# A hybrid layer in one kernel: the pass boundary rewritten (held mLSTM outputs, kept tiles chosen by chain state, output weights through the weight ring, attention banks dealt anew)

## The chip, the cores and the metric

The kernel runs on 1 core of a Trainium2 chip. The metric is the device time of one execution in microseconds. A profiled execution also leaves a trace of the five engines: TensorE (PE, with its weight loads shown as PEld), VectorE (DVE), ScalarE (ACT), GpSimd (POOL), and SyncE (SP), which here only issues DMA transfers. L243 means line 243 of the kernel's file.

## The reference

One layer over 2,048 positions of width 1,024, all in float32. The input is normalised, and one projection gives the columns of three head groups. Each group's output is gated; the three are joined, projected back, added to the input, and normalised.

```
hn = rmsnorm(x, norm_g)
z  = einsum('bsd,de->bse', hn, w_in)            # split among three groups
att   = band_chunk_attention(aq, ak, av, rel_bias)   # 6 heads, own 64-chunk and 8 before it
y_a   = att * silu(ag)
h_ml  = mlstm_chunkwise(silu(conv(mq)), silu(conv(mk)), mv, mi, mf)   # 6 heads, matrix memory
y_b   = sigmoid(mo) * head_rmsnorm(h_ml) * silu(mg)
h_gla = gla_chunkwise(gq, gk, gv, log_alpha)         # 4 heads, gated linear attention
y_c   = head_rmsnorm(h_gla) * silu(gg)
x     = x + einsum('bse,ed->bsd', concat(y_a, y_b, y_c), w_out)
return rmsnorm(x, final_g)
```

The mLSTM group carries a matrix state from chunk to chunk. Its output is divided by a normaliser, normalised per head, and multiplied by the gate `gm` (sigmoid(mo) * silu(mg)).

## The kernel before, in words

**Arithmetic.** Large products use split operands: each float32 operand is held as a high part (a rounded `fp32r` copy, made by ACT) and a low part (the difference, made by DVE or POOL), and three matmuls stand for one: high x high, high x low, low x high. So a projection tile (`proj_g`, L239) is 8 x 3 = 24 matmuls of 128x128 against 512 columns, L243 to L245. `load_w` (L229) brings one tile's weights through the raw ring `wraws` (2 buffers of 512 KB) into the split ring `wring` (5 buffers).

**Pass A** (L757 to L788) walks over four blocks of 512 positions. Each block projects in a fixed order: `gq`, `gk`, two groups of four `proj_t` tiles with `gg` between, six tiles for the mLSTM's q and k (`proj_m`), six for its gates (`proj_gm`), and nine for attention (`proj_a`: q, k and gate, three each). Attention's q, k, v and gate go to DRAM (`q_d`, `k_d`, `v_d`, `ga_d`), and so do the outputs of mLSTM and GLA (`y_d`, row tiles 3 to 7).

TensorE's order is written out by the program. Between the projection's matmuls it calls `flow.piece(12 * 0.227)`, and the planner `Flow` (L33) then steps the chains that are due: generators that issue some TensorE work and yield its cost and the gap after which the next step is due. `flow.need(name)` steps chains with no projection between, until the named one has ended. The other engines' order is chosen by the compiler's scheduler, across the whole program.

The chain `mlstm` (L521) handles four chunks of 128 positions per block. Per chunk: decay matmuls (L532, cost 0.7, gap 4.5), scores and key transposes (L542, L546; 1.0, gap 4.5), then output and state update (L560, L565, L577), the normalisation on DVE and POOL (L589 to L602; 1.7, gap 9), and last the output's transposes (L611) and the product with `gm` (L613), then the store L614 (0.35, gap 1). The next chunk begins only after that. In the last block, attention tiles 5 to 8 are not projected but kept (L507); then `need("gla")` and `need("mlstm")` (L787) finish the chains.

**Pass B** (from L791). `attention(q)` yields steps of `scores` (L844: per row tile up to two segments, L868, then the masked sum and row minimum on DVE, L882, the exponential on ACT, L885, the scaling on POOL, L887) and of `mix` (L901: transposes L932 into bank `tp`, the high and low copies `ph` L937 and `pl` L938, and the products with v, L946 and L949, in bank `w`, evacuated by L953 and L954). `merge` interleaves two generators in a given ratio. The mix of a head lags its scores by two heads in block 0 and by one later.

`proj_kept` (L512) projects the four kept tiles between the first 32 steps of block 0's attention. Then `load_wo` (L812) closes the projection's pools, opens the pool `late` on the same memory, and loads the output weights in 16 halves with four raw buffers, together with block 0's row tiles 3 to 7 of y; each is split by L839 (ACT) and L840 (DVE or POOL). Its 21 steps alternate with the 28 that remain of block 0's attention.

After that, for blocks 1 to 3, `spread` mixes the attention of block q with `out_mm(q - 1)` (L978): 64 pieces of three matmuls (L990 to L992), then residual and final norm. Block 1's attention takes its first eight steps alone. At the end of a block `load_y` (L1010, L1012) loads the next five row tiles through the four raw buffers and splits them (L897, L898). `out_mm(3)` runs alone at the end.

PSUM has eight banks: in pass B two each for `s`, `tp`, `w` and `ip`.

Of the kernel before, what the change touches and what calls it, by code (L numbers as in the profile page):

```python
# [104 lines left out]
def trunk_kernel(ctx: ExitStack, tc: tile.TileContext, xT, x, w_f, w_t, w_o, w_gates, norm_g, conv_w,  # L105
# [36 lines left out]
    with ExitStack() as pa_:  # L142
# [378 lines left out]
        def mlstm(q, qk, vs, R):  # L521
            rt, iwl = R["rt"], R["iwl"]
            for c in range(NC):
# [77 lines left out]
                hb = m_tile([P, 3, 2, 64])  # L601
                nc.vector.tensor_tensor(hb.rearrange("p a b d -> p b a d"), ov[:, :, :, 0:64],  # L602
                                        sm[:, 3].unsqueeze(3).broadcast_to([P, 2, 3, 64]), op=ALU.mult)
                hf = hb.rearrange("p a b d -> p (a b d)")
                yield 1.7, 9.0 if c < NC - 1 or q == NQ - 1 else 17.0
                while "gm" not in R:
                    yield 0.0, 1.0
                gm = R["gm"]
                ht_ps = bank("mt")
                for p in range(3):  # L610
                    nc.tensor.transpose(out=ht_ps[:, p * P:(p + 1) * P], in_=hf[:, p * P:(p + 1) * P], identity=ident)  # L611
                hbt = m_tile([P, 3, P])
                nc.vector.tensor_tensor(hbt, ht_ps[:, 0:384].rearrange("p (a t) -> p a t", a=3), gm[:, :, cs], op=ALU.mult)  # L613
                nc.sync.dma_start(y_d[q, :, 3:6, cs], hbt)  # L614
                yield 0.35, 1.0
# [141 lines left out]
        for q in range(NQ):  # L757
# [19 lines left out]
            flow.start("mlstm", mlstm(q, qk, vs, M))  # L777
# [9 lines left out]
        flow.need("gla")  # L787
        flow.need("mlstm")  # L788


    with ExitStack() as pb_:  # L791
# [4 lines left out]

        def pbank(tag):
            return (psum_i if tag == "ip" else psum).tile([P, 512], FP32, name=tag)
# [11 lines left out]
        late = {}  # L810

        def load_wo(Y):  # L812
            lag = []
            pg_.close()
            late["p"] = ctx.enter_context(tc.tile_pool(name="late", bufs=2, reuse_waits="tile"))
            late["fg"] = fg = late["p"].tile([P, D], FP32, name="fg", bufs=1)
            wo = late["wo"] = {}
            for j in range(2):
                for k in (3, 4, 5, 6, 7, 0, 1, 2):
                    raw = late["p"].tile([P, 512], FP32, name="wraw", bufs=4)  # L820
                    nc.sync.dma_start(raw, w_o[k][:, 512 * j:512 * j + 512])
                    w = wo[k, j] = late["p"].tile([P, 2, 512], FR, name="wo", bufs=2 * KT)
                    lag.append((w, raw, other()))
                    if len(lag) > 2:
                        split_late(*lag.pop(0))
                    yield
                    if j == 0 and k >= 3:
                        raw = late["p"].tile([P, QT], FP32, name="wraw", bufs=4)
                        nc.sync.dma_start(raw, y_d[0, :, k, :])
                        Y[k] = y_tile(k)  # L830
                        lag.append((Y[k], raw, nc.gpsimd))
                        split_late(*lag.pop(0))
                        yield
            for e in lag:
                split_late(*e)
            nc.sync.dma_start(fg, final_g.partition_broadcast(P))
# [7 lines left out]
        def scores(q, h, out_):  # L844
# [13 lines left out]
            for tt in range(NC):  # L858
# [7 lines left out]
                for l in range(2):  # L866
                    for sp, (c0, cn) in zip(sps, segs):
                        nc.tensor.matmul(sp[:, :cn], qq[:, l, tt * P:(tt + 1) * P], kk[:, ko + c0:ko + c0 + cn],  # L868
                                         start=(l == 0), stop=(l == 1))
                if q == 0:  # L870
# [21 lines left out]
        def y_tile(k):  # L892
            return (big if k < 3 else late["p"]).tile([P, 2, QT], FR, name="y", bufs=6 if k < 3 else 5)

        def split_y(src, k):
            yk = y_tile(k)
# [4 lines left out]
        def mix(q, h, Y, vv, pts, nkb):  # L901
# [39 lines left out]
            def pv(pr, pp, g, pk, last, ph, pl):  # L941
                if g == 0:
                    ops[pr] = pbank("w")
                op = ops[pr]
                for e, (b, use, w) in enumerate(pk):
                    nc.tensor.matmul(op[:, use[0] * P:use[0] * P + P * len(use)], vv[:, b, :], ph[:, w:w + P * len(use)],  # L946
                                     start=(g == 0 and e == 0), stop=False, skip_group_check=True)
# [3 lines left out]
                if last:  # L951
                    ps_ = slice(pr * ST, (pr + 1) * ST)
                    nc.scalar.copy(cc[mr, ps_], op[cr, :ST])  # L953
                    nc.vector.tensor_tensor(cc[mr, ps_], op[mr, :ST], cc[mr, ps_], op=ALU.add)  # L954

            held = []
            for it in todo:
                ph, pl = turn_(*it)
                yield
                if held:  # L960
                    pv(*held.pop())
                    yield
                held.append(it + (ph, pl))
            pv(*held.pop())
            if h % 2 == 1:
                nc.gpsimd.tensor_tensor(cc, cc, gt, op=ALU.mult)
                Y[h // 2] = split_y(cc, h // 2)
            yield

        def attention(q, Y):  # L970
            lag, nb = (2, 6) if q == 0 else (1, 14)
            done = []
            for h in range(AH + lag):
                a = scores(q, h, done) if h < AH else None
                b = mix(q, h - lag, Y, *done[h - lag]) if h >= lag else None
                yield from merge(a, b, NC, nb)

        def out_mm(q, Y):  # L978
            wo, fg = late["wo"], late["fg"]
            for tt in range(NC):  # L980
                t = slice(tt * P, (tt + 1) * P)
                ts_ = slice(q * QT + tt * P, q * QT + (tt + 1) * P)
                xr = late["p"].tile([P, D], FP32, name="xr", bufs=2)
                nc.sync.dma_start(xr, x[ts_, :])
                sm = big.tile([P, 4], FP32, name="sm4")
                for j in range(2):
# [9 lines left out]
                    jk = late["p"].tile([P, 512], FP32, name="jk", bufs=1)  # L996
# [122 lines left out]
```

## Time and profile before

| what | us |
|---|---|
| median of 3 runs | 1363.43 (1361.69 to 1365.0) |
| profiled execution | 1360.25 |
| its span on the core | 1358.5 |
| DVE busy in the span | 815.6 |
| ACT busy in the span | 600.7 |
| POOL busy in the span | 628.4 |
| start of the output product of block 0 | 1017.94 |

The span is the time between the first and last instruction that the trace shows; the execution's own time lies 1.75 us above it. The page cuts the span into 40 slices of 34 us and gives each engine's busy share in tenths, and the TensorE clock that was granted:

```profile
PE   4999999999999999999999999996979999999997
PEclk7999999999999999999999999997959999989999
```

Slices are counted from 0. Slices 27 to 29 (918 to 1020 us) are the boundary between the passes; the first and the last slice are the start and the end of the kernel.

### The profile page before, as it was taken

To read this page: it belongs to the slowest core of one execution; us is meant where nothing else is said; L and a number is where in the kernel's file an instruction comes from. 1 tells how busy PE (TensorE), PEld (TensorE's weight loads), DVE (VectorE), ACT (ScalarE), POOL (GpSimd) and SP (SyncE) were. 2 spreads that over 40 slices of the span, in tenths; PEclk is the share of its full clock that TensorE was granted. 3 is DMA by queue.
4 is the path that set the end of the run, shared out by engine and by line. 5 is a ranking of instruction groups with operands and counts; after the bars stand their busy time and mean duration, and the time that the engine had idled before them with its cause. 6 is when DMAs were issued, how large, how long until landed. Compare 5 with 4: busy or idle time off the path is not lost.

```text
span 1358.5 us, 19994 instructions
## 1 busy us (share of the span) xinstructions
PE 1289.8 (95%) x7044; PEld 1045.6 (77%) x7044; DVE 815.6 (60%) x1886; ACT 600.7 (44%) x1149; POOL 628.4 (46%) x847
## 2 busy tenths in 40 slices
PE   4999999999999999999999999996979999999997
PEld 2787878877777888778787877885758877877886
DVE  6626656573866575475768356555657756656631
ACT  5624332563523274342336344222566645645531
POOL 5236751333964244468333476522364353454442
PEclk7999999999999999999999999997959999989999
DMA  7444224624323563422352642332695554464222
GB/s 244 151 125 138 83 88 134 230 74 139 109 77 109 138 215 113 133 76 82 125 137 68 189 135 70 99 104 80 173 285 176 173 174 150 142 192 132 78 86 77
DMA packets 107204, 180.09 MB, mean 133 GB/s; under 512 B 9824, under 2 KB 54752, under 8 KB 107104
## 3 DMA queue, kind: packets, MB, share of 16 engines
q1 hardware_dynamic: 102496, 170.43, 41.6%
q10 hardware_dynamic: 4608, 8.39, 1.7%
q8 instruction: 55, 0.90, 0.3%
q14 instruction: 45, 0.37, 0.1%
HBM read 143.14 MB, written 35.65 MB: 132 GB/s over the span
## 4 chain that ended last, share of the span: by engine, by line
PE 76%; DVE 10%; DMA 5%; ACT 4%; issue 3%; POOL 2%; SPq 0%; POOLq 0%; DVEq 0%; ACTq 0%
PE ip L243 13%; PE ip L245 12%; PE ip L244 12%; PE ip L263 3%; PE ip L265 3%; PE ip L264 3%; PE ip L992 3%; PE ip L990 3%; PE ip L991 3%; PE s L868 3%; PE tp L932 2%; DVE pt L882 2%; PE ga L696 2%; PE w L949 2%; PE s L565 1%
## 5 line engine op out<-in xcount | busy, mean ns | idle before, releaser
L243 PE MATMUL ip<-x,w 128*128 128x512 f32 x800 | 328.0, 410 | 0.0
L245 PE MATMUL ip<-x,w 128*128 128x512 f32 x800 | 313.5, 392 | 0.0
L244 PE MATMUL ip<-x,w 128*128 128x512 f32 x800 | 312.7, 391 | 0.0
L243 PEld LDWEIGHTS ip<-x,w 128*128 128x128 f32 x800 | 150.7, 188 | 43.2 <-issue 13.9
L245 PEld LDWEIGHTS ip<-x,w 128*128 128x128 f32 x800 | 150.4, 188 | 33.2
L244 PEld LDWEIGHTS ip<-x,w 128*128 128x128 f32 x800 | 150.9, 189 | 29.6 <-issue 2.2
L236 DVE TENSOR_TENSOR w<-wraw,w 128x1024 fp32r<-128x1024 f32 x88 | 123.2, 1400 | 81.3 <-ACT w L235 80.8
L235 ACT CAST w<-wraw 128x1024 fp32r<-128x1024 f32 x132 | 138.0, 1046 | 67.1 <-DMA wraw<-in_w_t 30.7
L236 POOL TENSOR_TENSOR w<-wraw,w 128x1024 fp32r<-128x1024 f32 x44 | 106.8, 2428 | 80.5 <-ACT w L235 80.5
L887 POOL TENSOR_SCALAR pt<-pt,sm 128x640 f32<-128x640 f32 (+2 forms) x96 | 70.4, 735 | 146.4 <-DVE sm L886 115.3
L990 PE MATMUL ip<-wo,y 128*128 128x512 f32 x256 | 106.6, 416 | 0.0
L263 PE MATMUL ip<-w,x 128*128 128x512 f32 x256 | 101.3, 396 | 4.2 <-ACT vg L427 4.2
L885 ACT ACTIVATE pt<-pt,sm 128x640 f32<-128x640 f32 (+2 forms) x96 | 73.3, 763 | 69.6 <-DVE sm L882 67.1
L656 POOL TENSOR_TENSOR prd<-gk,zg 128x16 f32<-128x16 f32 (+15 forms) x128 | 73.8, 576 | 64.0 <-PE pw L662 57.8
L992 PE MATMUL ip<-wo,y 128*128 128x512 f32 x256 | 101.1, 395 | 0.3 <-POOL y L898 0.3
L991 PE MATMUL ip<-wo,y 128*128 128x512 f32 x256 | 101.1, 395 | 0.0
L265 PE MATMUL ip<-w,x 128*128 128x512 f32 x256 | 99.8, 390 | 0.0
L264 PE MATMUL ip<-w,x 128*128 128x512 f32 x256 | 99.7, 390 | 0.0
L938 DVE TENSOR_TENSOR pl<-tp,ph 128x512 fp32r<-128x512 f32 (+2 forms) x126 | 74.6, 598 | 31.3 <-ACT ph L937 29.9
L868 PE MATMUL s<-kk,qq 128*128 128x384 f32 (+1 forms) x360 | 81.5, 335 | 10.0 <-DVE sm L882 7.9
L868 PEld LDWEIGHTS s<-kk,qq 128*128 128x128 f32 x360 | 60.8, 202 | 29.2 <-DVE sm L882 23.2
L398 ACT ACTIVATE e<-ip 128x512 f32<-128x512 f32 x44 | 26.2, 594 | 126.5 <-PE ip L245 108.1
(244 smaller groups left out, 2445.1 us busy)
## 6 DMA issues: line engine op xcount, KB each, us to landing
wraw<-in_w_f SPq DMA_DIRECT2D x100, 512.0 KB, 3.6
wraw<-in_w_t SPq DMA_DIRECT2D x32, 512.0 KB, 3.7
qq<-q_d SPq DMA_DIRECT2D x48, 256.0 KB, 4.3
kk<-k_d SPq DMA_DIRECT2D x18, 512.0 KB, 6.4
vv<-v_d SPq DMA_DIRECT2D x18, 512.0 KB, 7.2
xraw<-in_x SPq DMA_DIRECT2D x16, 512.0 KB, 5.1
xraw<-in_xT SPq DMA_DIRECT2D x16, 512.0 KB, 6.8
xr<-in_x SPq DMA_DIRECT2D x16, 512.0 KB, 3.7
```

What stands on the lines that cost most here:

```text
L235: nc.scalar.copy(w[:, :, 0, :], rv)
L236: other().tensor_tensor(w[:, :, 1, :], rv, f32(w[:, :, 0, :]), op=ALU.subtract)
L243: nc.tensor.matmul(ps, w[:, k, 0, :], X[k][:, 0, :], start=(k == 0), stop=False)
L244: nc.tensor.matmul(ps, w[:, k, 0, :], X[k][:, 1, :], start=False, stop=False)
L245: nc.tensor.matmul(ps, w[:, k, 1, :], X[k][:, 0, :], start=False, stop=(k == KT - 1))
L263: nc.tensor.matmul(ps, X[k][:, 0, t], w[:, 0, :], start=(k == 0), stop=False)
L264: nc.tensor.matmul(ps, X[k][:, 0, t], w[:, 1, :], start=False, stop=False)
L265: nc.tensor.matmul(ps, X[k][:, 1, t], w[:, 0, :], start=False, stop=(k == KT - 1))
L868: nc.tensor.matmul(sp[:, :cn], qq[:, l, tt * P:(tt + 1) * P], kk[:, ko + c0:ko + c0 + cn], start=(l == 0), stop=(l == 1))
L990: nc.tensor.matmul(ps, Y[k][:, 0, t], wo[k, j][:, 0, :], start=(e == 0), stop=False)
L991: nc.tensor.matmul(ps, Y[k][:, 0, t], wo[k, j][:, 1, :], start=False, stop=False)
L992: nc.tensor.matmul(ps, Y[k][:, 1, t], wo[k, j][:, 0, :], start=False, stop=(e == KT - 1))
```

## The change

1. In the last block the chain `mlstm` no longer ends chunks 0 to 2 with the output's transposes. It puts the normalised output, now in a tile of the ring `g`, on a list, yields with a gap of 3.0, and goes on with the next chunk. A new chain `mlstm_out` (`held_out`) issues the transposes, the product with `gm` and the store for each held chunk, 8.0 after the chunk is there. Chunk 3 does its own.
2. Which attention tiles are kept in the last block is no longer fixed: a tile is kept if one was kept before it or if no chain is live.
3. The output weights are loaded through `wraws` (eight loads of 512 KB, and three of y tiles) into buffers of `wring` (row tiles 3 to 7) and `xs` (0 to 2). The projection's pools stay open; `late` is a small pool of its own. The final norm's weights go to two tiles of `ev`. The y tiles sit in a fixed list `ys`, in part on buffers of `ev` and `xs`. `load_y` uses the two buffers of `wraws`.
4. PSUM in pass B: two banks for `s`, three for `tp`, one for `w`, two for `ip`. Both halves of a head's product share the one `w` bank and are evacuated together. In `scores` each segment's two matmuls come together, with a step's end between segments. In `mix` the products lag the transposes by two turns instead of one.
5. Block 0's attention alternates scores and mix steps 6 to 6; the last two mixes run beside the scores of block 1's head 0, which block 1 then need not do. Block 1's eight steps alone are gone.

```
         def proj_a(q, X):
             for b, name in enumerate(A_TILES):
-                if q == NQ - 1 and b >= 5:
+                if q == NQ - 1 and (kept or not flow.chains):
                     kept.append((b, name))
                     continue
...
+        def mlstm_out(q, hf, cs, R):
+            while "gm" not in R:
+                yield 0.0, 1.0
+            gm = R["gm"]
+            ht_ps = bank("mt")
+            for p in range(3):
+                nc.tensor.transpose(out=ht_ps[:, p * P:(p + 1) * P], in_=hf[:, p * P:(p + 1) * P], identity=ident)
+            hbt = m_tile([P, 3, P])
+            nc.vector.tensor_tensor(hbt, ht_ps[:, 0:384].rearrange("p (a t) -> p a t", a=3), gm[:, :, cs], op=ALU.mult)
+            nc.sync.dma_start(y_d[q, :, 3:6, cs], hbt)
+            yield 0.35, 1.0
+
+        def held_out(q, held, R):
+            for c in range(NC - 1):
+                while len(held) <= c:
+                    yield 0.0, 1.0
+                yield 0.0, 8.0
+                yield from mlstm_out(q, *held[c], R)
...
-                hb = m_tile([P, 3, 2, 64])
+                late_ = held is not None and c < NC - 1
+                hb = g_tile([P, QT])[:, 0:384].rearrange("p (a b d) -> p a b d", a=3, b=2) if late_ else m_tile([P, 3, 2, 64])
...
+                if late_:
+                    held.append((hf, cs))
+                    yield 1.7, 3.0
+                    continue
                 yield 1.7, 9.0 if c < NC - 1 or q == NQ - 1 else 17.0
...
+                yield from mlstm_out(q, hf, cs, R)
...
+        NB = {"s": 2, "tp": 3, "w": 1, "ip": 2}
...
-            pg_.close()
-            late["p"] = ctx.enter_context(tc.tile_pool(name="late", bufs=2, reuse_waits="tile"))
...
+            for n, k in enumerate((3, 4, 5, 6, 7, 0, 1, 2)):
+                raw = wraws.tile([P, D], FP32, name="wraw")
+                nc.sync.dma_start(raw, w_o[k])
+                if n < 5:
+                    w = wring.tile([P, 2 * D], FR, name="w").rearrange("p (l n) -> p l n", l=2)
+                    wo[k, 0], wo[k, 1] = w[:, :, 0:512], w[:, :, 512:1024]
+                    put(w, raw, other())
+                else:
+                    for j in range(2):
+                        w = wo[k, j] = xs.tile([P, 2, 512], FR, name="x")
+                        put(w, raw[:, 512 * j:512 * j + 512], other())
+                yield
...
-                for l in range(2):
-                    for sp, (c0, cn) in zip(sps, segs):
+                for sp, (c0, cn) in zip(sps, segs):
+                    for l in range(2):
...
+                    if sp is not sps[-1]:
+                        yield
...
-                if last:
-                    ps_ = slice(pr * ST, (pr + 1) * ST)
-                    nc.scalar.copy(cc[mr, ps_], op[cr, :ST])
-                    nc.vector.tensor_tensor(cc[mr, ps_], op[mr, :ST], cc[mr, ps_], op=ALU.add)
+                if last and pr == NC // 2 - 1:
+                    nc.scalar.copy(cc[mr], ops[0][cr])
+                    nc.vector.tensor_tensor(cc[mr], ops[0][mr], cc[mr], op=ALU.add)
...
-                if held:
-                    pv(*held.pop())
+                held.append(it + (ph, pl))
+                if len(held) > 2:
+                    pv(*held.pop(0))
                     yield
...
+        def attention0(Y, nxt):
+            done = []
+            for h in range(AH):
+                b = mix(0, h - 2, Y, *done[h - 2]) if h >= 2 else None
+                yield from merge(scores(0, h, done), b, 6, 6)
+            yield from merge(scores(1, 0, nxt), two(mix(0, AH - 2, Y, *done[AH - 2]), mix(0, AH - 1, Y, *done[AH - 1])), 8, 12)
+
+        def attention(q, Y, done):
+            for h in range(len(done), AH + 1):
                 a = scores(q, h, done) if h < AH else None
-                b = mix(q, h - lag, Y, *done[h - lag]) if h >= lag else None
-                yield from merge(a, b, NC, nb)
+                b = mix(q, h - 1, Y, *done[h - 1]) if h else None
+                yield from merge(a, b, 8, 14)
...
-            raw = late["p"].tile([P, QT], FP32, name="wraw", bufs=4)
+            raw = wraws.tile([P, D], FP32, name="wraw")[:, 0:QT]
```

More of the change, by code (lines that the diff above doesn't have):

```diff
@@ L809, in trunk_kernel @@
         nc.gpsimd.memset(mz[64:128, 0:64], NEG)
-        late = {}
+        latep = ctx.enter_context(tc.tile_pool(name="late", bufs=1, reuse_waits="tile"))
+        wo = {}
+        fgs = []
+        ys = [big.tile([P, 2, QT], FR, name="y", bufs=6) for _ in range(6)]
+        ys.append(latep.tile([P, 2, QT], FR, name="y"))
         def load_wo(Y):
             lag = []
-            pg_.close()
-            late["p"] = ctx.enter_context(tc.tile_pool(name="late", bufs=2, reuse_waits="tile"))
[L816 to L825, printed above, removed]
-                    yield
-                    if j == 0 and k >= 3:
-                        raw = late["p"].tile([P, QT], FP32, name="wraw", bufs=4)
[L829 to L833, printed above, removed]
@@ L834, in load_wo @@
             for e in lag:
                 split_late(*e)
-            nc.sync.dma_start(fg, final_g.partition_broadcast(P))
+            for j in range(2):
+                fg = ev.tile([P, QT], FP32, name="e")
+                nc.sync.dma_start(fg, final_g[512 * j:512 * j + 512].partition_broadcast(P))
+                fgs.append(fg)
         def split_late(w, raw, eng):
@@ L890, in scores, with y_tile, split_y @@
             out_.append((vv, pts, nk // P))
[L892 to L896, printed above, removed]
+        def y_tile(q, k):
+            if len(ys) == 7 and (k == 7 or k < 3 and q == 1):
+                ys.extend(ev.tile([P, 2, QT], FR, name="hl") for _ in range(2))
+            if len(ys) == 9 and k < 3 and q == 1:
+                ys.extend(xs.tile([P, 2, QT], FR, name="x") for _ in range(2))
+            if k >= 3:
+                return ys[(0, 1, 2, 6, 7)[k - 3]]
+            return ys[3 + k if q % 2 == 0 else 8 + k]
+        def split_y(src, q, k):
+            yk = y_tile(q, k)
             nc.scalar.copy(yk[:, 0, :], src)
@@ L982, in out_mm @@
                 ts_ = slice(q * QT + tt * P, q * QT + (tt + 1) * P)
-                xr = late["p"].tile([P, D], FP32, name="xr", bufs=2)
+                xr = latep.tile([P, D], FP32, name="xr", bufs=2)
                 nc.sync.dma_start(xr, x[ts_, :])
@@ L1010, in load_y @@
         def load_y(q, Y, k):
-            raw = late["p"].tile([P, QT], FP32, name="wraw", bufs=4)
+            raw = wraws.tile([P, D], FP32, name="wraw")[:, 0:QT]
             nc.sync.dma_start(raw, y_d[q, :, k, :])
-            Y[k] = split_y(raw, k)
+            Y[k] = split_y(raw, q, k)
         YN = 4 * 2 * KT
         YA = {}
-        first = attention(0, YA)
+        nxt = []
+        first = attention0(YA, nxt)
         for _ in proj_kept(X):
@@ L1025, in trunk_kernel @@
             YB = {}
-            att = attention(q, YB)
-            if q == 1:
-                for _ in range(8):
-                    next(att)
-            spread(att, 7 * 14 + 4 * 6, out_mm(q - 1, YA), YN)
+            units = AH + 1 - len(nxt)
+            spread(attention(q, YB, nxt), units * 14 + 8 * (units - 1), out_mm(q - 1, YA), YN)
+            nxt = []
             YA = YB
```

62 lines of the change are left out of this document (34 added, 28 removed).

## The prediction

> **What bounds the kernel now.** I read the page's first part, then a table of stages that I cut myself around the pass boundary, then TensorE's timeline at the cuts.
>
> ```profile
> span 1358.5 us, 19994 instructions
> PE 1289.8 (95%) x7044; PEld 1045.6 (77%) x7044; DVE 815.6 (60%) x1886; ACT 600.7 (44%) x1149; POOL 628.4 (46%) x847
> ```
>
> TensorE is busy 95% of the span, so only its idle and slow-clock time can be won. The stage table (PE, PEld, DVE, ACT and POOL busy us, granted clock, DMA share, GB/s) shows where that time sits:
>
> ```profile
> 910.32:917.88 7.56, 6.86 (x64) 5.93 (x62) 5.92 (x18) 2.00 (x4) 1.01 (x1) 1.00 0.29 72
> 923.72:932.71 8.99, 8.24 (x42) 7.41 (x42) 4.41 (x12) 0.84 (x1) 0.00 (x0) 0.56 0.07 22
> 938.37:974.85 36.48, 35.92 (x199) 30.09 (x197) 20.04 (x82) 17.61 (x50) 10.07 (x18) 0.95 0.60 165
> 974.85:1002.73 27.88, 19.43 (x105) 15.79 (x104) 15.98 (x50) 17.89 (x43) 13.86 (x15) 0.77 0.93 264
> 1002.73:1017.94 15.21, 11.81 (x38) 8.06 (x37) 10.66 (x32) 10.28 (x22) 11.26 (x11) 0.50 0.95 279
> 938.37:1017.94 79.57, 67.15 (x339) 53.95 (x337) 46.68 (x164) 45.78 (x112) 35.19 (x44) 0.80 0.78 221
> ```
>
> The cuts come from TensorE's timeline (start, us, what; in brackets the idle time before and who ended it):
>
> ```profile
> 908.26 0.39 PE L243 MATMUL ip<-x,w 128*128 128x512 f32 x1
> 908.95 0.39 PE L243 MATMUL ip<-x,w 128*128 128x512 f32 x1
> ...
> 910.32 0.78 PE L532 MATMUL s<-hl_nm,sel 128*128 128x128 f32 x6
> ...
> 923.72 0.90 PE L611 MATMUL mt<-ident,m 128*128 128x128 f32 x3 [5.84 <-DVE m L602]
> ...
> 937.85 0.87 PE L611 MATMUL mt<-ident,m 128*128 128x128 f32 x3 [5.14 <-DVE m L602]
> 938.37 0.77 PE L243 MATMUL ip<-x,w 128*128 128x512 f32 x1
> ...
> 1017.94 0.78 PE L990 MATMUL ip<-wo,y 128*128 128x512 f32 x1
> ```
>
> Three stages follow each other. From 910.32 to 938.37 the last mLSTM chunks run with nothing beside them: two waits of 5.84 and 5.14 us for the output's normalisation, and the clock down to 0.56. From 938.37 to 974.85 the four kept projection tiles cover the first attention steps. From 974.85 to 1017.94 attention of block 0 runs alone against the loads of the output weights, at a DMA share of 0.93 to 0.95 and a clock that ends at 0.50. Only then does the output product start.
>
> **Part one: the mLSTM tail.** I stepped the planner with the costs and gaps in the code through the last block. With the old code it gives the order that the trace has at 910.32 (five tiles done, then the chain alone). With the new code a chunk costs 0.7 + 4.5 + 1.0 + 4.5 + 1.7 + 3.0 = 15.4 planner us instead of 22.75, and the held outputs run as a chain of their own. The mLSTM chain fires its last step just before the last of the nine tiles and is retired 1.0 planner us later, inside that tile. So at each test a chain is still live: all nine tiles are projected in pass A, and **the list of kept tiles stays empty**. The four tiles that covered attention now cover the mLSTM tail.
>
> The tail lasts 938.37 - 910.32 = 28.05 us. Its TensorE work stays: 6.86 us, then 8.24 us at 0.56 of the clock, which is 4.6 at full, and 0.3 for the last transposes, 11.8 together. That frees 16.2 us. The shorter gap of 3.0 us before the next chunk, and the bank `mt` shared with the held outputs, can give some back; between nothing and 3 us I take 0.5, since the planner leaves 2.7 us or more between two users of that bank. **Gain 15.7 us.** The held tiles lie in a ring that the gates no longer use, and their three `y_d` writes, which stand on SP among the `k_d` and `ga_d` writes, are wanted only by the last block's output: both cost nothing, and if a write held SP up, the next weight load behind it has four tiles of time.
>
> **Part two: attention of block 0, now alone.** A projection matmul starts every (908.95 - 908.26) / 3 = 0.23 us, so the four tiles' 96 are 22.1 us. Of the 79.57 us between 938.37 and 1017.94, 57.5 remain. They also hold two row tiles of scores and three mix steps of block 1 that now come later, beside the output product: some 3.8 us at full clock (half of the last row's rest, below). To be beaten: **53.7 us**. What will stand there? Call it T: scores and mixes of six heads, and the first head of block 1. The clock first: with little work the array went to 0.50, and these rows show steps there, the last two one group at full clock:
>
> ```profile
> 992.58 1.08 PE L932 MATMUL tp<-ident,pt 128*128 128x128 f32 x6
> 998.41 0.80 PE L946 MATMUL w<-ph,vv 128*128 128x128 f32 x2 [4.75 <-ACT ph L937]
> ...
> 1002.73 1.27 PE L868 MATMUL s<-kk,qq 128*128 128x384 f32 x4
> 1004.45 1.75 PE L868 MATMUL s<-kk,qq 128*128 128x384 f32 x4 [0.45 <-DVE sm L882]
> ...
> 1042.19 0.74 PE L868 MATMUL s<-kk,qq 128*128 128x384 f32 x4
> 1042.77 0.40 PE L990 MATMUL ip<-wo,y 128*128 128x512 f32 x1
> ```
>
> A mix at half clock is 1.08 + (1002.73 - 998.41) = 5.4 us, less a short wait 5.3. A row tile of scores in a late block (1,280 columns) takes 1042.77 - 1042.19 = 0.58 us at full clock, so from 1.16 to the 1.75 us of the row at 1004.45 at half clock; six of those 1.75 fill 10.5 of the 15.2 us before 1017.94, and half of the rest and of two such tiles is the 3.8 above. A head of block 0 has 2,560 columns: 2.3 to 3.5 us, I take 2.7; block 1's first head has four row tiles, 4.6 to 7 us, I take 6. T on TensorE = 6 x (5.3 + 2.7) + 6 = 54 us at half clock. It starts at full clock, which saves about 2. Waits come on top: in the last two stages TensorE idled (27.88 - 19.43) + (15.21 - 11.81) = 11.9 us, without the one of 4.75 us some 7 in 38; with the longer lag I take half of that rate, 5 us. **T = 57.** From below it is held by DVE and ACT, which did 46.7 and 45.8 us in the old stage of nearly the same work, so T is at least 46. From above:
>
> ```profile
> 997.24 0.62 ACT L839 CAST wo<-wraw 128x512 fp32r<-128x512 f32 x1 [4.05 <-DMA wraw<-in_w_o]
> DMA to landing us min/median/max: 2.5/4.9/11.9
> L235 ACT CAST w<-wraw 128x1024 fp32r<-128x1024 f32 x132 | 138.0, 1046 | 67.1 <-DMA wraw<-in_w_t 30.7
> L236 DVE TENSOR_TENSOR w<-wraw,w 128x1024 fp32r<-128x1024 f32 x88 | 123.2, 1400 | 81.3 <-ACT w L235 80.8
> ```
>
> The second line is that of the old output-weight loads (L821). In the old code they could start only after the last projection, as their pool lay on the projection's memory. The new ones take the projection's own rings: raw buffers are free some four tiles before pass A ends, and each finished tile frees a weight buffer. Yet there are eleven raw loads through two buffers. With a landing of 7 us for 512 KB (my estimate, between the 4.9 and 11.9 of 256 KB loads), a copy of 1.05 and a subtract of 1.4, two take 9.5, eleven 52 us, two or three of them ahead of the stage. That hides within T. On SP a raw load that waits for its buffer holds back `qq`, `kk` and `vv` loads of the next heads, and on ACT a weight copy that waits holds back `ph`, as the 4.05 us show; a few us of that are in T. **Part two costs 57 - 53.7 = 3.3 us**; with T from 46 to 70 it is from +7.7 to -16.3.
>
> **Part three: the steady attention.** TensorE's waits from 1018 to the end:
>
> ```profile
> PE s L868 <- DVE sm L882: 5.3, 15, 1.2
> PE w L946 <- ACT ph L937: 3.5, 9, 0.6
> PE w L949 <- DVE pl L938: 1.9, 6, 0.5
> ```
>
> One score segment per step, a third `tp` bank and two turns of lag aim at these 10.7 us. I take 6 as won. The single `w` bank adds a wait: the next head's first product needs the copy and the add of the last one. Three turns and some scores and output pieces lie between, about 4 us, so 0 to 0.5 us in each of 18 heads; I take 2. Behind that wait on TensorE stand the scores and output pieces of the same order.
>
> The y loads of blocks 1 to 3 lose two of four raw buffers. Before, at the last boundary:
>
> ```profile
> 1301.84 0.62 ACT L897 CAST y<-wraw 128x512 fp32r<-128x512 f32 x1 [1.30 <-PE ip L992]
> 1302.54 1.29 POOL L898 TENSOR_TENSOR y<-wraw,y 128x512 fp32r<-128x512 f32 x1 [0.62 <-ACT y L897]
> 1305.04 5.05 POOL L898 TENSOR_TENSOR y<-wraw,y 128x512 fp32r<-128x512 f32 x4
> DMA to landing us min/median/max: 2.7/3.0/4.0
> 1310.15 0.50 PE L992 MATMUL ip<-wo,y 128*128 128x512 f32 x1 [0.28 <-POOL y L898]
> ```
>
> Here the fifth tile alone waited for a buffer, and was 0.28 us late. With two buffers the third load starts when the first split ends (1303.83), the fourth at 1306.3; they land 3.0 later, and the fifth starts only after the third's split, 1308.8, lands 1311.8, is copied and subtracted by 1313.7. The product could have used that tile at 1310.15 - 0.28 = 1309.9, so it is 3.8 us late, 3.5 more than before. At the two earlier boundaries attention lies between the pieces: about 1.2 each. Sum for part three: 6 - 2 - 5.9 = **-2 us**, between -9 and +8.
>
> **Sum:** 15.7 - 3.3 - 2 = 10.4 us. The profiled run took 1360.25 us (span 1358.5); 10 less is 1350. The median of the runs shown is 1363.43, 3.2 above that run, so I forecast **1353**.
>
> **Rivals.** *The clock comes back* (0.22). One segment per step removes the 0.45 us wait before each score group, so TensorE at half clock would run without a gap, return to full, and T fall to the DVE floor, about 48: gain 15.7 + 5.7 - 2 = 19, time 1344. For: the stage from 938.37 has a mean clock of 0.95, that is 3.6 us at half before dense work freed it. Against: at 0.50 with TensorE 78% busy it did not return for 15 us. The Trainium skill, "TensorE: Matmul & The Clock Gate", Part 1, says that about 3.4 us of sustained work give the full clock and an idle window of that length takes it away; the 3.6 us agree. Its Part 4 says that transposes do not count as busy for the clock, which no run here shows and which would speak against this rival.
>
> *The ring of two* (0.17, slower). If loads share a crowded DMA and each raw waits for a split that is itself queued, the weights come too late: at a landing above about 10 us eleven loads take (10 + 2.45) / 2 x 11 = 68 us, and T passes 67.4, where the sum turns negative (15.7 + 53.7 - 2). With the 11.9 us of the slowest old load and the SP queue held, T is near 80: 1376. For: 0.78 x 79.57 = 62 us of DMA time lay in the old stage. Against: loads that start before the stage.
>
> *No change* (0.09): T from 65 to 70, the cover lost costs just what the tail gives.
>
> **Numbers.** My forecast's own case, T from 50 to 64, has 0.52: 1346 to 1360. With the rivals' nearer halves the range is 1337 to 1368. Below 0.2% (2.7 us) a measurement of this kernel can't tell a change. Faster 0.74, same 0.09, slower 0.17.
>
> **What would show it.** No L243 after the first L868 of pass B; TensorE without a wait over 1 us for L602 before it; the last projection near 944. Then a stage of 50 to 64 us at a clock of 0.5 to 0.7 until the first L990. First `in_w_o` load before the last projection ends. L868's wait for L882 mostly gone; waits of some 4 us for L897/L898 ahead of the last output block. I am wrong if kept tiles remain, if the clock stays at 1.0 in that stage, or if ACT stands for raw weights for more than 10 us in it.

## The result and the profile after

The changed kernel takes 1329.70 us (median of 4 runs, 1327.89 to 1334.69), the kernel before on the same chip 1363.1 us (1361.69 to 1365.0). The ratio is 0.9763 [0.9737, 0.9788]. The forecast was 1353, with a range from 1337 to 1368: the direction was right, the gain is 33 us instead of 10. The profiled execution took 1327.89 us, of which the span is 1326.2. The difference of the two profiled spans, 1358.5 - 1326.2 = 32.3 us, is the sum that the prediction's terms have to make.

By the page of after TensorE is busy for 1270.6 us, 96% of the span; the share rose by one point and tells nothing of the cause. TensorE's timeline of after gives the places of the cuts (start, us, what, and in brackets the idle time and who ended it):

```profile
938.85 0.49 PE L527 MATMUL mt<-ident,m 128*128 128x128 f32 x3
...
944.42 0.40 PE L245 MATMUL ip<-x,w 128*128 128x512 f32 x1
944.65 1.64 PE L903 MATMUL s<-kk,qq 128*128 128x128 f32 x8
...
955.94 0.66 PE L903 MATMUL s<-kk,qq 128*128 128x128 f32 x2 [4.41 <-DMA kk<-k_d]
```

The mLSTM's output transposes (L527) lie between projection matmuls, with no wait for the normalisation in front. The last projection (L245) and the first attention scores (L903) meet at 944.65, where the prediction said "near 944": no tile is kept. The same stage table for after, cut there and at the first output product, L1042 at 1000.80 (us; then PE, PEld, DVE, ACT, POOL busy; granted clock, DMA share, GB/s):

```profile
910.93:938.85 27.92, 27.92 (x152) 23.57 (x152) 12.40 (x33) 3.79 (x8) 8.94 (x13) 1.00 0.77 220
938.85:944.65 5.80, 5.80 (x28) 4.84 (x27) 1.15 (x2) 0.60 (x1) 0.00 (x0) 1.00 0.65 194
944.65:1000.80 56.15, 38.71 (x224) 32.65 (x223) 38.81 (x146) 40.01 (x97) 35.16 (x40) 0.82 0.93 250
1000.80:1326.20 325.40, 310.16 (x1831) 268.42 (x1830) 188.65 (x548) 170.30 (x370) 149.67 (x153) 0.98 0.49 144
```

The mLSTM tail, in which TensorE idled for 5.84 and 5.14 us, is now full at a clock of 1.00. The stage of block 0's attention is one step, busy 38.71 of 56.15 us. The last row has to be set beside the same stretch of before, the steady part from its first output product to the end:

```profile
1017.94:1358.50 340.56, 320.02 (x1814) 267.72 (x1812) 195.33 (x562) 172.73 (x386) 148.26 (x151) 0.98 0.45 139
```

It went from 340.6 to 325.4 us, though it took over some of block 1's work. That is most of the surprise. The prediction put the work that moved at 3.8 us. The trace shows less: 18 matmuls more start in the steady part of after than in that of before, two of scores, ten transposes and six products with v. In before the transposes and the products stand just ahead of the cut:

```profile
1013.82 1.91 PE L932 MATMUL tp<-ident,pt 128*128 128x128 f32 x8
1015.97 1.01 PE L946 MATMUL w<-ph,vv 128*128 128x128 f32 x3 [0.24 <-ACT ph L937]
1017.17 0.69 PE L949 MATMUL w<-pl,vv 128*64 128x128 f32 x3 [0.20 <-DVE pl L938]
1017.66 0.63 PE L932 MATMUL tp<-ident,pt 128*128 128x128 f32 x2
```

They take 4.1 us with 0.44 of waits, at half clock, so 1.8 at full; the two score matmuls add 0.3. An estimate of 2 us is used from here on, and 55.5 us in place of the prediction's 53.7 for the stage of block 0 in before without its kept tiles and this work.

Which waits went? The prediction read TensorE's waits from its matmul rows. The rows of the weight loads (PEld) tell another story. First the waits of before from 1017.94 to the end, then those of after from 1000.80 to the end (what waits, and for whom; us in total, times, longest):

```profile
PEld s L868 <- DVE sm L882: 15.2, 29, 1.6
PEld w L949 <- DVE pl L938: 7.4, 22, 0.7
PEld w L946 <- ACT ph L937: 7.3, 10, 1.1
PEld ip L992 <- POOL y L898: 1.0, 2, 0.7
```

```profile
PEld ip L1044 <- POOL y L941: 3.3, 3, 1.5
PEld s L903 <- DVE sm L919: 2.7, 4, 1.3
PEld ip L1042 <- ACT y L940: 2.0, 1, 2.0
PEld w L992 <- DVE pl L981: 1.9, 5, 0.5
PEld tp L975 <- POOL pt L924: 1.1, 1, 1.1
PEld ip L1044 <- POOL hl L941: 1.1, 2, 0.6
PEld w L989 <- ACT ph L980: 0.2, 1, 0.2
```

Before there were 30.9 us of waits, not the 10.7 of the matmul rows, and 12.3 are left. The reason for the two figures stands in before's timeline, first by the matmul rows, then by the weight-load rows:

```profile
1108.56 0.44 PE L868 MATMUL s<-kk,qq 128*128 128x384 f32 x1
1109.19 0.68 PE L868 MATMUL s<-kk,qq 128*128 128x256 f32 x3 [0.20 <-DVE sm L882]
...
1111.53 0.44 PE L868 MATMUL s<-kk,qq 128*128 128x384 f32 x1 [0.96 <-DVE sm L882]
```

```profile
1109.19 0.42 PEld L868 LDWEIGHTS s<-kk,qq 128*128 128x128 f32 x3 [0.45 <-DVE sm L882]
...
1111.53 0.19 PEld L868 LDWEIGHTS s<-kk,qq 128*128 128x128 f32 x1 [1.39 <-DVE sm L882]
```

One wait, two sizes: 0.20 and 0.45 us, 0.96 and 1.39. A score matmul's row lasts 0.44 us, though without a wait four of them start within 0.58 us (the prediction's rows at 1042.19 and 1042.77), one every 0.15. So a row goes on past the point from which the next matmul could start. A wait that begins under this tail is shown too short by it, by 0.25 and 0.43 us in these rows, and one shorter than the tail isn't shown. The Trainium skill, "Perfetto Trace Analysis", section "Tensor Engine Instruction (MATMUL, LD_WEIGHTS)", says that the profiler works out the end of a TensorE instruction from its size instead of observing it; rows that last longer than the distance between two starts fit that. The prediction's three rows had 30 waits with 10.7 us; here the same three have 61 with 29.9.

### The profile page after: what moved, and what is told of

The parts are those of the page before. It is cut to its first block, busy times and chain, and to the rows that moved or that the text cites. A ratio compares the mean times of both kernels' runs of the same rounds, so it can differ in the third digit from the quotient of the medians.

```text
span 1326.2 us, 19917 instructions
## 1 busy us (share of the span) xinstructions
PE 1270.6 (96%) x7044; PEld 1039.6 (78%) x7044; DVE 803.8 (61%) x1859; ACT 593.8 (45%) x1120; POOL 629.8 (47%) x845
## 4 chain that ended last, share of the span: by engine, by line
PE 74%; DVE 9%; POOL 5%; DMA 4%; ACT 4%; issue 3%; SPq 0%; POOLq 0%; DVEq 0%; ACTq 0%
PE ip L243 11%; PE ip L245 11%; PE ip L244 11%; PE ip L1044 4%; PE ip L1042 4%; PE ip L1043 4%; PE ip L263 3%; PE ip L265 3%; PE ip L264 3%; PE s L903 3%; PE tp L975 3%; PE w L992 2%; PE w L989 2%; PE ga L711 2%; PE s L584 1%
## 5 line engine op out<-in xcount | busy, mean ns | idle before, releaser
L245 PE MATMUL ip<-x,w 128*128 128x512 f32 x800 | 313.0, 391 | 0.0
L245 PEld LDWEIGHTS ip<-x,w 128*128 128x128 f32 x800 | 150.3, 188 | 33.1
L924 POOL TENSOR_SCALAR pt<-pt,sm 128x640 f32<-128x640 f32 (+2 forms) x96 | 72.6, 759 | 109.6 <-DVE sm L923 88.4
L903 PE MATMUL s<-kk,qq 128*128 128x256 f32 (+2 forms) x360 | 86.2, 328 | 13.9 <-DMA kk<-k_d 5.8
L981 DVE TENSOR_TENSOR pl<-tp,ph 128x512 fp32r<-128x512 f32 (+2 forms) x126 | 74.0, 597 | 18.8 <-ACT ph L980 17.2
L903 PEld LDWEIGHTS s<-kk,qq 128*128 128x128 f32 x360 | 61.9, 200 | 23.3 <-DVE sm L919 8.4
L668 POOL TENSOR_TENSOR gk<-gk,al 128x16 f32<-128x16 f32 (+14 forms) x120 | 74.7, 623 | 9.8 <-ACT al L646 2.6
L980 ACT CAST ph<-tp 128x512 fp32r<-128x512 f32 (+2 forms) x126 | 62.6, 512 | 36.8 <-PE tp L975 35.1
L468 DVE SCALAR_TENSOR_TENSOR qk<-u,cw,qk 128x512 f32<-128x512 f32 x72 | 69.3, 963 | 9.8 <-ACT qk L466 8.3
```

Of the source, the lines that this page charges most:

```text
L245: nc.tensor.matmul(ps, w[:, k, 1, :], X[k][:, 0, :], start=False, stop=(k == KT - 1))
L668: nc.gpsimd.tensor_tensor(b16(gk)[:, :, 0:c], b16(gk)[:, :, 0:c], b16(al)[:, :, c:c + 1].broadcast_to([P, NB, c]), op=ALU.mult)
L981: nc.vector.tensor_tensor(pl[:, :wd], tp[:, :wd], f32(ph[:, :wd]), op=ALU.subtract)
```

## The experiments

My theory after the result: the steady part gained because waits for the two `s` banks and for `ph` and `pl` went, and the waits are as large as the weight-load rows say. Rivals: the matmuls themselves run closer (order of the operands, clock, traffic); the lag and the third `tp` bank do it, and not the score segments; the boundary did more than I saw. For each kernel I also take its steady part less its PEld waits: by the theory it is the same in all. The kernel before in these runs had medians of 1362.47 to 1364.46.

**Which half.** The changed boundary with the old attention (the edits of the next two experiments together), and the old boundary with the new attention (the planner's counts follow in both; not shown):

```
e1, on after:  both edits of the next pair
e2, on before: NB = {"s": 2, "tp": 3, "w": 1, "ip": 2}; segments outside, a yield between;
               one w bank; if len(held) > 2; merge(a, b, 6 if q == 0 else 8, nb)
```

> The changed kernel, with the attention's new order undone: both segments of a row tile in one step, two tp banks, two w banks, a lag of one turn, old merge ratios. The pass boundary stays new. Theory A (the missing 20 us lie in the steady attention of blocks 1 to 3, in waits that TensorE's weight loads show and its matmul row did not): 1345 to 1350 us, and the weight loads' waits for L919, L980 and L981 from the first output piece to the end back near the old 30 us. Rival B (the boundary itself is worth 30 us, for instance because the loads of the output weights no longer reach into block 1): 1330 to 1336 us. What I had forecast for this part (2 us of loss for the whole attention and y part): 1327 to 1332.

> The kernel before, with the attention's new order alone: one segment per step, banks 2/3/1/2, a shared w bank, a lag of two turns, new merge ratios; old boundary, four kept tiles, old load of the output weights. Theory A: 1343 to 1348 us, and weight-load waits from 1018 us on down from 30 to under 8 us. Rival B: 1357 to 1363 us.

The old attention behind the new boundary took 1352.2 us, 0.9914 [0.9892, 0.9936]: 11.7 below before, and a little above the theory's 1345 to 1350. By profiled spans it is 7.7 (1358.5 - 1350.8), since before's profiled run lies 3.2 us under its median; the stage of block 0 takes 63.0 us, 7.5 above the 55.5 to be beaten, and the tail's 15.8 less that leave 8.3. The new attention alone took 1337.58 us, 0.9804 [0.9785, 0.9823]: 26.3 below, and below all that was expected of it. By profiled spans this second gain is 22.9 us, 12.6 of them in the steady part (340.6 to 328.0) and 10.3 ahead of it (first output product at 1007.63 instead of 1017.94; 2 of the 10.3 are the work that moves behind the cut here too). Whether the halves add to the whole can't be told: by medians they make 38.0 us against 33.4, by profiled spans 30.6 against 32.3. The boundary didn't do more than I saw. The waits in the steady part of the first of these kernels are those of before (30.3 us in all, led by these):

```profile
PEld s L903 <- DVE sm L917: 14.2, 27, 1.9
PEld w L990 <- DVE pl L979: 6.2, 17, 0.8
PEld w L987 <- ACT ph L978: 5.4, 7, 1.1
```

**Which part of the attention.** The score segments as before (and the planner's counts for them), with the new banks and lag kept; and the banks and lag as before, with the new segments:

```
e3: -                for sp, (c0, cn) in zip(sps, segs):
    -                    for l in range(2):
    +                for l in range(2):
    +                    for sp, (c0, cn) in zip(sps, segs):
    -                    if sp is not sps[-1]:
    -                        yield
    ...
e4: -        NB = {"s": 2, "tp": 3, "w": 1, "ip": 2}
    +        NB = {"s": 2, "tp": 2, "w": 2, "ip": 2}
    ...
    -                if len(held) > 2:
    +                if len(held) > 1:
    ...
```

> The changed kernel with only the segments undone: both segments' four matmuls in one step, merge ratios adapted; the three tp banks, one w bank and the lag of two turns stay. Theory A: the weight loads' wait for L919 returns to about 12 to 15 us, the time is 1336 to 1342. If the lag alone carried the gain, 1329 to 1333.

> The changed kernel with only the lag and the banks undone: a lag of one turn, two tp and two w banks; one segment per step stays. Theory A: the waits for L980 and L981 return to 10 to 15 us, the time is 1336 to 1342. If the segments alone carried the gain, 1329 to 1333.

1345.9 us, 0.9869 [0.9849, 0.9890], and 1339.42 us, 0.9819 [0.9801, 0.9836], against 0.9763 of after; the first is slower than either expectation had it. Steady part and stage of block 0: 338.9 and 62.5 us with the old segments, 327.1 and 65.5 with the old lag, 325.4 and 56.15 with neither undone. By these profiles the segments are worth 13.5 us in the steady part and 6 in the stage; the lag and the third bank only 1.7 in the steady part, but 9 in the stage. Two limits to this: the profile of the old segments lies 2.7 us above that kernel's median, and the parts don't add, since with the old segments the old lag costs the stage next to nothing (63.0 against 62.5 us). The waits of both in the steady part, in this order:

```profile
PEld s L903 <- DVE sm L917: 17.3, 29, 1.9
PEld w L987 <- ACT ph L978: 3.1, 7, 0.7
PEld w L990 <- DVE pl L979: 2.4, 7, 0.5
```

```profile
PEld w L992 <- DVE pl L981: 4.3, 14, 0.5
...
PEld w L989 <- ACT ph L980: 1.7, 4, 0.6
PEld s L903 <- DVE sm L919: 1.1, 3, 0.7
```

The segments remove the wait for the softmax (L917 or L919) ahead of the scores, which the lag alone leaves at 17.3 us. The waits for `ph` and `pl`, 11.6 us with the old attention, fall by half with either part, to 5.5 and 6.0, and to 2.1 with both.

**Why the segments do it.** If TensorE waits for a free bank, a third `s` bank under the old segments should remove that wait as well; `tp` gives the bank up. And if what counts is how much other work lies between two uses of a bank, the pairwise order without the yield should bring only part:

```
e11, on e3: NB = {"s": 3, "tp": 2, "w": 1, "ip": 2}
e12, on e3: -                for l in range(2):
            -                    for sp, (c0, cn) in zip(sps, segs):
            +                for sp, (c0, cn) in zip(sps, segs):
            +                    for l in range(2):
```

> The changed kernel with the segments undone (both segments' four matmuls in one step, alternating between two banks), but three banks for the scores and two for the transposes. Theory W (the step waits until the score banks of the step before are read): one bank is free at once, so the weight loads' wait for the score reduction in the steady part falls from 17 us to 5 to 9, the time from 1346 to 1336 to 1341. Rival O (the alternating order of four matmuls costs by itself): the wait row may fall, the time stays 1344 to 1348.

> The changed kernel with both segments in one step, but in the new order (a segment's two matmuls together) and with the new banks. Theory W (the space between segments is what counts): 1341 to 1347 us, the wait for the score reduction 10 us or more. Rival O (the alternating order counts): 1329 to 1334 us.

The third `s` bank: 1354.53 us, 0.9941 [0.9924, 0.9958]. The wait for the softmax fell from 17.3 to 3.6 us, as a wait for a bank must. The kernel is slower all the same, by 8.6 us where some 5 to 10 of gain were expected, since the bank it took was needed:

```profile
PEld tp L973 <- DVE pl L979: 23.0, 18, 3.2
...
PEld s L903 <- DVE sm L917: 3.6, 10, 0.9
```

With a lag of two turns and two `tp` banks, the transposes of a third turn wait until `pl` (L979) has left the bank. So the third `tp` bank goes with the longer lag. The pairwise order without the yield: 1340.59 us, 0.9835 [0.9806, 0.9864], steady part 332.0, between 338.9 and 325.4; its wait:

```profile
PEld s L903 <- DVE sm L917: 12.8, 20, 2.6
```

The order brings 6.9 us of the steady part and the spacing 6.6; of the wait for the softmax the order takes 4.5 us and the spacing 10.1. The split is rough, as this kernel's four runs lie up to 9 us apart. In both cases no instruction of the scores was removed, only the point where TensorE comes back to a bank.

Steady part and PEld waits of these kernels, and their difference (us):

| kernel | steady part | PEld waits | difference | matmul-row waits |
|---|---|---|---|---|
| before (+2 moved work) | 342.6 | 30.9 | 311.7 | 11.0 |
| after | 325.4 | 12.3 | 313.1 | 6.9 |
| old attention | 343.5 | 30.3 | 313.2 | 11.8 |
| new attention alone | 328.0 | 14.3 | 313.7 | 8.2 |
| old segments | 338.9 | 27.2 | 311.7 | 11.6 |
| old lag | 327.1 | 16.2 | 310.9 | 6.6 |
| three `s` banks | 348.4 | 36.1 | 312.3 | 23.5 |
| pairs in one step | 332.0 | 20.3 | 311.7 | 8.5 |

The steady part moves by 23 us over these, the difference by 3. (A second profile of after gives 324.4, 12.6 and 311.8, so 1.3 us of that is the spread of one kernel.) The matmul rows don't carry it: 11.8 and 8.5 stand for steady parts that lie 11.5 us apart. The rival that the matmuls run closer by themselves has 3 us left.

**What sets the stage of block 0** (56.15 us). In TensorE's waits of this stage, by the matmul rows of after, loads stand beside the chain of softmax and splits:

```profile
PE s L903 <- DMA kk<-k_d: 5.8, 2, 4.4
PE w L992 <- DVE pl L981: 4.6, 7, 1.8
PE s L903 <- DVE sm L919: 3.6, 6, 1.6
PE s L903 <- DMA qq<-q_d: 2.4, 1, 2.4
```

Three kernels take loads away. The first reads 64 of the 1,024 columns of each output weight row and repeats them, so it leaves out most of that load and its output weights are other ones; the copies and subtracts stay. The second loads `kk` of two heads at once, so that three of six loads come earlier. The third does both, and ran beside a second measurement of after:

```
e13: -                nc.sync.dma_start(raw, w_o[k])
     +                nc.sync.dma_start(raw[:, 0:64], w_o[k][:, 0:64])
     ...
     -                    put(w, raw, other())
     +                    put(w, raw[:, 0:64].unsqueeze(1).broadcast_to([P, 16, 64]), other())
     ...
e8:  -            kk = early.tile([P, 1024], FR, name="kk")
     +            hk = 512 * (h % 2) if q == 0 else 0
     +            if hk == 0:
     +                cur["kk"] = early.tile([P, 1024], FR, name="kk")
     +                for i in range(2 if q == 0 else 1):
     +                    dma.dma_start(f32(cur["kk"][:, 512 * i:512 * i + nk]), k_d[h + i, :, :, kb:kb + nk].rearrange("l d t -> (l d) t"))
     ...
e15: both            e16: after, unchanged
```

> The changed kernel, but each of the eight output-weight loads brings 64 of 1,024 columns (32 KB instead of 512 KB), which are repeated over the tile: the output product uses wrong weights. Copies, subtracts and TensorE's work are the same; 3.8 MB of loads are gone. Theory L (loads set the 56 us of block 0's attention): that stage falls to 44 to 49 us, the time by as much, to 1318 to 1324. My prediction's theory (TensorE at half clock sets it, 54 us of work): the stage stays 53 to 56 us, the time 1327 to 1331.

> The changed kernel, but in block 0 the keys of two heads are loaded together into the two halves of one buffer, so that four heads' keys are in flight instead of two; the bytes are the same. If the single late loads hold the stage (kk waits of 5.8 us): stage 50 to 53 us, time 1323 to 1327. If the bandwidth of all loads holds it: the stage moves by under 1.5 us, time 1328 to 1331.

> The changed kernel with both relief of loads at once: keys of two heads per load, and output-weight loads of 32 KB that are repeated over the tile (wrong weights in the output product). If late loads of any kind set the 56 us of block 0's attention, they can no longer take each other's place: stage 44 to 49 us, time 1317 to 1322. If the chain of TensorE, ACT and DVE sets it (each alone gave 54 and 56 us): stage 52 to 56 us, time 1325 to 1329.

> The changed kernel itself, on the same chip as the run beside it: 1328 to 1332 us, a stage of 55 to 58 us from the first scores to the first output piece. It gives the spread of that stage between two profiles of one kernel.

Small output weights: 1326.27 us, 0.9733 [0.9711, 0.9754], stage 54.0. `kk` in pairs: 1328.84 us, 0.9746 [0.9728, 0.9764], stage 56.2; the wait for `kk` went and others grew in its place, those for `qq` from 2.4 to 4.6 us, for `ph` from 0.2 to 4.2 and for the softmax from 3.6 to 4.7. Both: 1323.66 us, 0.9715 [0.9698, 0.9731], stage 50.8. After again: 1329.23 us, 0.9763 [0.9744, 0.9782], stage 57.8. The stage with both, then that of after measured again (columns as in the stage table):

```profile
944.31:995.09 50.78, 36.72 (x224) 30.25 (x222) 40.74 (x146) 39.89 (x97) 33.83 (x40) 0.87 0.73 198
```

```profile
945.48:1003.28 57.80, 41.09 (x224) 35.87 (x222) 39.14 (x146) 40.13 (x97) 35.17 (x40) 0.76 0.91 244
```

The result lies between the two expectations. Relief of both kinds takes 5 to 7 us off the stage (against 56.15 and 57.80), the small output weights alone 2 to 4, and the pairs alone nothing; the two profiles of after lie 1.65 apart. In the remaining 51 TensorE still waits 3.1 us for `qq`; TensorE, DVE and ACT are each busy some 37 to 41 us, so none of them alone is the bound; that they hand work to one another in turn is the likely reading, and it wasn't tested further.

**The cover traded.** By the planner's rule no tile is kept. Keeping the last four (the number of before) or the last two gives cover back to the attention and takes it from the mLSTM tail; and the y tiles can be loaded in pairs, against the waits for L940 and L941:

```
e5:  -                if q == NQ - 1 and (kept or not flow.chains):
     +                if q == NQ - 1 and b >= 5:
e6:  +                if q == NQ - 1 and b >= 7:
e7:  -            for k in (3, 4, 5, 6, 7):
     -                load_y(q, YA, k)
     +            for ks in ((3, 4), (5, 6), (7,)):
     +                load_y(q, YA, ks)
     ...
     -            nc.sync.dma_start(raw, y_d[q, :, k, :])
     +            nc.sync.dma_start(raw, y_d[q, :, ks[0]:ks[-1] + 1, :])
e14: e6 and e7
```

> The changed kernel with the old rule for kept tiles: four projection tiles go back beside block 0's attention, the held mLSTM outputs stay. The planner then has 13 us of its own time with no projection at the end of pass A (37 before the change). If the stage of block 0's attention is a fixed 56 us of small waits between engines, four tiles put into those waits shorten the sum: tail 5 to 9 us longer, stage with 22 us of tiles in it 60 to 66 us: 1317 to 1327 us. If the stage is TensorE at half clock, as I predicted, the tiles bring the clock up and the gain is at the upper end. If the tail's waits cost what they save: 1328 to 1333.

> The changed kernel with two kept tiles (the last two). The planner has 4.3 us without a projection. First theory as for four kept tiles: tail 2 to 4 us longer, stage about 58 us with 11 us of tiles in it: 1319 to 1325 us. Second (cover and tail cancel): 1328 to 1332.

> The changed kernel with the y tiles of blocks 1 to 3 loaded in pairs (3 loads for 5 tiles, so that four tiles fit the two raw buffers again). My prediction's price for the smaller ring was 5.9 us in all; the weight loads' waits for L940 and L941 are 6.4 us. They should fall under 2 us, and the time by 3 to 6, to 1324 to 1327. If the splits on POOL hold them and not the ring: 1329 to 1331.

> The changed kernel with both: two kept tiles and the y tiles in pairs. If the two are independent, the sum of what each brings: 1314 to 1322 us.

Four kept tiles: 1336.77 us, 0.9802 [0.9785, 0.9819], another result than expected. TensorE waits at the end of pass A again, as its timeline shows:

```profile
931.68 0.69 PE L758 MATMUL gb<-ident,n 128*128 128x128 f32 x2 [7.56 <-DVE n L753]
934.56 0.87 PE L527 MATMUL mt<-ident,m 128*128 128x128 f32 x3 [2.19 <-DVE m L622]
```

The second bracket is the mLSTM's normalisation. The first, the larger one, is the GLA's last output (L753): GpSimd (POOL) is on the attention's bias tiles (L827) from 924.70 for 5.47 us, and only at 930.14 comes to a small instruction that this output needs (L752). The stage is 64.73 us with 93 projection matmuls, some 21 us, in it, so some 43.5 without: nearly 13 less than after. But the kept tiles hold the weight ring, so that the output weights come later, and in the first 10 us of the output product, which are full in after, TensorE is busy for 5.87:

```profile
936.51:1001.24 64.73, 56.16 (x316) 47.64 (x315) 38.26 (x144) 37.86 (x92) 27.01 (x36) 0.89 0.75 210
1001.24:1011.24 10.00, 5.87 (x37) 4.73 (x36) 5.57 (x13) 5.70 (x12) 7.67 (x6) 1.00 0.85 260
```

Two kept tiles: 1326.15 us, 0.9725 [0.9708, 0.9742], stage 60.67 with some 10 of projection; the first 10 us of its output product have TensorE at 8.34. The y tiles in pairs: 1331.52 us, 0.9760 [0.9742, 0.9779], no gain: the waits for the y splits fell from 6.4 to 3.9 us, and that for `pt` (L924) in the same stretch rose from 1.1 to 2.8, so this expectation missed. Its steady part is 323.0 us, 1.4 to 2.4 below the two profiles of after, but its stage 58.3. Both together: 1325.85 us, 0.9717 [0.9693, 0.9741], no sum of gains either. The kernels with two kept tiles are the fastest that compute everything, some 0.4% below after; the intervals just touch.

## Why the prediction was right in direction and wrong in size

**Part one, the mLSTM tail: right.** Forecast +15.7 us. From the old start of pass B less its kept tiles to the new one: 938.37 + 22.1 - 944.65 = **+15.8**. No tile is kept and the waits for the normalisation are gone; with four tiles kept again, 2.19 us of them and 7.56 for the GLA's output stood there.

**Part two, the stage of block 0: the sum right, its composition not.** Forecast T = 57 and -3.3; measured 56.15, so 55.5 - 56.15 = **-0.65**. The 53.7 us to be beaten were too few: the prediction took 3.8 us as moved where some 2 moved. It read six groups of scores in before's last row, which has five, and its own terms, half of 4.7 and of 3.5, make 4.1. The prediction made T of 52 us of TensorE work, nearly all at half clock, and 5 of waits. Measured: 38.7 busy at a mean clock of 0.82, and 17.4 idle. Too slow a clock and too few waits cancelled each other, by luck. The step "I take half of that rate, 5 us" fell: the longer lag does help, by the 9 us that the old lag costs here, but the waits of a stage that runs alone are far more than 5. The output weights were in time, as the prediction had it: the first output weights were asked for at 904.02, ahead of the last projection, and ACT waited 4.3 us in all for `in_w_o` in the stage. It was the loads of `kk` and `qq` that TensorE stood for, 8.2 us in all.

**Part three, the steady attention: here the prediction failed.** Forecast -2; measured 340.6 + 2 - 325.4 = **+17.2**. The failing step is "aim at these 10.7 us. I take 6 as won": the 10.7 us were read from matmul rows, and the same waits are 29.9 us by the weight-load rows (15.2 + 7.4 + 7.3). After has 4.8 of them left (2.7 + 1.9 + 0.2), so 25.1 were won. The other terms: the y loads were forecast at -5.9 and show 6.4 (3.3 + 2.0 + 1.1) where 1.0 was, so -5.4, about right. The single `w` bank, forecast at -2, shows no wait worth a row in the steady part. A wait of the transposes for `pt` costs 1.1. Together 25.1 - 5.4 - 1.1 = 18.6, against 17.2; the 1.4 between them lie within the 3 us that the table's differences scatter.

15.8 - 0.65 + 17.2 = 32.35, the 32.3 us of the two spans. The three parts have to make that, as they cut the same two spans; the estimate of the work that moved only shifts between the second and the third.

**The rivals.** *The ring of two* did not occur as a bound: the loads began before the stage. Late loads hold only the 5 to 7 us above. *The clock comes back* did, in part (below), but T did not fall to 48, since idle time took its place. *No change* rested on a T of 65 to 70. With the old lag T was 65.5 and the kernel still 24 us below before, since the steady part gained; even with the old attention and its 63.0 the boundary gained.

Left open: what exactly sets the last 51 us of the stage.

## What to carry to other kernels

Size TensorE's waits from the weight-load rows, not from the matmul rows: many short waits before matmuls of 0.2 us are nearly invisible in the latter and were here 30 us instead of 11. Where TensorE alternates between two PSUM banks that another engine empties, put other work between two uses of a bank before asking for a third one: the same matmuls, one segment per step, saved some 11 to 13.5 us, while a third bank taken from the transposes cost more than it gave. Cover that is moved from one bare stretch to another is worth what the two stretches wait for, and a split between them was the fastest here, if by little.

## What the hardware showed that was not expected

The prediction let the clock stay at half through a stage with little work, since before it stood at 0.50 for 15 us with TensorE 78% busy. In after it did not (two rows of the stage table's kind, 5 us each, and TensorE's timeline between them):

```profile
980.00:985.00 5.00, 4.79 (x30) 4.59 (x31) 3.64 (x17) 2.96 (x8) 4.09 (x5) 0.69 0.97 257
985.00:990.00 5.00, 2.88 (x20) 2.23 (x20) 2.99 (x12) 3.58 (x10) 3.33 (x5) 1.00 1.04 315
```

```profile
980.12 0.58 PE L992 MATMUL w<-pl,vv 128*64 128x128 f32 x2 [1.82 <-DVE pl L981]
...
982.09 0.86 PE L975 MATMUL tp<-ident,pt 128*128 128x128 f32 x3
...
983.15 0.49 PE L975 MATMUL tp<-ident,pt 128*128 128x128 f32 x3
```

After 3 us without a wait from 980.12 on, three transposes take 0.49 instead of 0.86 us, and the clock is then 1.00 in a window with only 2.88 of 5 us busy. So the clock rose within the stage, and a low busy share right after did not take it away. In before's 15 us a wait of 0.45 to 0.7 us stood ahead of most groups of 1.75 (the prediction's row at 1004.45 is one), and the 78%, a mean over the whole stretch, said little against the rival.

What brings the clock back stays open. TensorE was busy for 2.98 of the 3.41 us from 979.69 to 983.10, at 0.50, and the clock rose; in before it was busy for 3.17 of the 3.41 us from 999.93, at 0.50, and the next 3.41 us were at 0.50 too. Nor is an unbroken run enough: in the kernel with the new attention alone, TensorE ran from 927.90 to 934.91 without a wait, on the mLSTM's smaller matmuls, at 0.50 throughout. The first half of that run:

```profile
928.40:931.80 3.40, 3.40 (x19) 2.90 (x18) 1.85 (x5) 0.84 (x1) 0.00 (x0) 0.50 0.00 0
```

The Trainium skill, "TensorE: Matmul & The Clock Gate", Part 1, names a window of about 3.4 us of sustained work; the 3 us from 980.12 are near it, and the 7 us of the other kernel show that such a run alone is not always enough. By its Part 4 the full clock does not engage for transposes; the three at 983.15, in a mix with other matmuls, do not bear that out, as they ran faster at a granted 1.00. Whether transposes count as work for the clock was not tested, and no experiment varied the gaps alone.
